# Windowed attention of a hybrid backbone: both key/value heads in one pass of 40 units, with the other input projections spread through it, and sinks in bfloat16

## The chip, the cores and the metric

One Trainium2 chip, one core of it. The metric is the device time of one execution in microseconds (us). In the text TensorE is PE (PEld for its weight loads), VectorE is DVE, ScalarE is ACT, GpSimd is POOL, and SyncE's queue, which issues every transfer here, is SP.

## The reference

512 latent tokens and 256 context tokens go through two layers of width 1024. Each layer is a SwiGLU block, a mixer and a second SwiGLU block, each behind an RMS norm with shift, scale and gate. The mixer of layer 0 is what the change is about: two kinds of attention side by side, from one input projection. Latent attention (MLA) has 8 heads; its queries, keys and values come from normalised low-rank latents through a second projection. Windowed attention has 8 query heads on 2 key/value heads; a latent query sees the context, the latent keys within 128 places and a "sink", one learned logit per head that takes part in the softmax alone:

```python
def attention_pair_mixer(h, hc, p, rope_mla, rope_win, ctx_out):
    z = h @ p["w_in"]
    ckv, kr, wk, wv, cq, wq = split_cols(z, PAIR_KV_SIZES + PAIR_Q_SIZES)
    ...
    k_a, v_a = mla_kv(ckv, kr, p, rope_mla)      # rms_norm(ckv) @ w_ukv; keys normalised per head
    o_a = dense_block_attention(mla_q(cq, p, rope_mla), ..., ...)   # rms_norm(cq) @ w_uq, norms, rotation
    o_b = window_block_attention(win_q(wq, p, rope_win), k_b, v_b, kc_b, vc_b, p["win_sink"])
    ...
# one block of window_block_attention:
    pr = softmax(concatenate([s_ctx, s_win, sink_col], axis=-1))
    o = pr[..., :n_ctx] @ vc + pr[..., n_ctx:n_ctx + 3 * BLOCK] @ vw      # the sink has no value
```

## The kernel before, in words

Nearly every product is a float32 product made of three float32r passes, so weights and operands are split into a high and a low part (`split`, L127 on ACT and L128 on DVE). Tokens stand in 6 tiles of 128: tiles 0 and 1 are context, 2 to 5 latent. The program is recorded in the order of the Python code and a scheduler of the tile layer then orders each engine's queue; each engine runs its own queue strictly in order, so where the scheduler puts an instruction decides what stands behind it.

`pair_mixer` (L715) is the mixer of layer 0. It first makes the window's keys and values and the first half of the queries, then goes through three stretches.

1. `att(0, ...)`: windowed attention of the four heads of key/value head 0. `win_attention` (L1078) makes a list of 20 units; a unit is a query tile of one head, or of two heads where the tile is context. `run_units` (L1020) issues, for unit i: the rest of unit i - 1's softmax (reciprocal L1032 on DVE, product L1035 on POOL), the "lanes" of other work, the scores of unit i, the transposes of unit i - 2's probabilities (L712), the products with the values that ended with unit i - 3 (L1158), then the copies out of PSUM (L1059, L1074), the row maximum (L1065, DVE) and the exponential (L1070, ACT). Two score buffers exist, so a pass starts and ends with units that overlap with few others.
2. `att(1, ...)`: the same for key/value head 1.
3. `mla_attention` (L1176): 40 units for the 8 latent heads. Its lane `rest` runs what is left of the query norms.

Between the units of each pass runs a background, cut in parts by `yield`: a generator tells what it has spent in its own unit of cost, and each attention unit is given a share, 3.2 in the first pass and 3.8 in the second. The first pass has `projections` (two column chunks of the input projection, norm and rotation of the second half of the window queries), the second has `latents` (L913: norms of the latents, their transposes, the products with `w_ukv` and `w_uq`, norm of the keys; its squares and its six products with 1/rms, L959, are on POOL) and the first of three `latent_queries` (L979: norm and rotation of the MLA queries of two token tiles, on DVE and POOL).

The sink enters the scores as one more product for each query tile and head, a single row of ones against two numbers of the sink row, in float32 (L1137):

```python
one = self.ones[0:1, :]
nc.tensor.matmul(out=s[:, n:n + 2], lhsT=one, rhs=sink[:, 4 * c + hd, :], start=True, stop=True)
```

There are 48 such products (24 of each key/value head), and the trace shows each as two TensorE instructions. `rsqrt` (L131) makes 1/sqrt of a small tile on DVE from a guess in integers and three Newton steps of three instructions, 11 in all; the kernel calls it 23 times, of which 8 are in this mixer. All its operands are in SBUF.

Of the kernel before, what the change touches and what calls it, by code (L numbers as in the profile page):

```python
# [8 lines left out]
F32 = mybir.dt.float32  # L9
# [13 lines left out]
T = SEQ + CTX  # L23
# [4 lines left out]
ALL_SEGS = [(0, 256), (256, 512), (512, T)]  # context tokens, latent tokens  # L28
# [3 lines left out]
class Stage:  # L32
    """A sub-layer: loads its first weights, one unit after the other, then waits for its operand."""
# [14 lines left out]
class Net:  # L48
# [28 lines left out]
    # ---- the residual: four slots that hold other things inside a mixer, while it waits in DRAM --  # L77
# [25 lines left out]
    def load_split(self, src, n, pool=None, keep=4, slots=(None, None)):  # L103
        """n columns in two halves, each as (hi, lo)"""
# [26 lines left out]
    def rsqrt(self, out, v, shape):  # L131
        """out = 1/sqrt(v) for a small positive float32 tile"""
# [3 lines left out]
        t = self.small.tile(shape, F32, tag="rs_t", name="rs_t", bufs=1)  # L136
        nc.vector.tensor_scalar(out=i, in0=v.bitcast(I32), scalar1=1, scalar2=None,
# [28 lines left out]
    def mod_finish(self, l, p):  # L166
        """bias; the scale piece becomes norm_g * (1 + scale), the FFN gates carry the 1/2"""
# [11 lines left out]
    def first_open(self, pool):  # L179
        """silu(c), silu(c_ctx) and zeros; the sum of four groups of 32 rows"""  # L180
# [14 lines left out]
    def first_product(self, pool, raw):  # L195
        """256 features of the vectors on the tensor engine, four products of 32 columns side by side"""
# [13 lines left out]
    def first_norm(self, pool, m, raw):  # L210
        """shift and scale of the first sub-layer, 128 features"""
# [7 lines left out]
    def first_gate(self, pool, i, raw):  # L219
        """half of the gate of the first sub-layer, 256 features"""  # L220
# [5 lines left out]
    def first_stats(self, pool):  # L226
        """1/rms of all tokens, on every partition"""
# [35 lines left out]
    def mod_half(self, i):  # L263
        """a half of silu(c) and of silu(c_ctx) on every partition, for the background products"""
# [35 lines left out]
    def norm_squares(self, pool, seg, order=range(KT)):  # L300
        """sum over the features of a partition of the squares"""
# [13 lines left out]
    def norm_stats(self, seg, acc):  # L315
        """1/rms of each token of the segment, on every partition (PSUM)"""
# [36 lines left out]
    def mm3(self, out, w, x, first, last):  # L353
        """out += w^T x, w = (hi, lo) stationary, x = (hi, lo) moving"""
# [17 lines left out]
    def regions(self, segs):  # L372
        """PSUM for two column tiles of each segment"""
# [72 lines left out]
    def ffn(self, l, sub, idx, segs, nxt, bg=(0, 0), first=4, start=False):  # L446
# [3 lines left out]
        # the first tiles: without the last segment, under the norm of it  # L450
# [9 lines left out]
        with st:  # L460
# [7 lines left out]
            def up(f, ss, regs=None):  # L468
                """the hidden tile f for the segments ss"""
# [13 lines left out]
            if start:  # L483
                # as the features come
# [61 lines left out]
    def seven_open(self, st, h, n0):  # L546
        """Gate and up columns (rows 1, 2) of a hidden tile against halves of the features and of the tokens,
        in seven products of halves in place of eight (Winograd's form of Strassen's)."""
# [50 lines left out]
        def start():  # L599
            """the place of the fourth block is free now"""  # L600
# [1218 lines left out]
```

## Time and profile before

| | us |
|---|---|
| device time, median of 3 runs (lowest, highest) | 2735.24 (2733.0, 2736.42) |
| span of the profiled execution, first to last instruction | 2731.1 |
| PE busy / DVE busy / ACT busy / POOL busy in that span | 2639.5 / 2171.2 / 1197.9 / 170.3 |
| mixer of layer 0, windowed attention: first score to first MLA score | 641 to 833 |
| mixer of layer 0, MLA attention | 833 to 958 |

The profiled execution's own device time is not among the three; its span stands 1.9 to 5.3 us under them, and 4.1 under their median. PE is busy 97% of the span, so nearly everywhere a microsecond counts only where PE's work gets shorter. The stretch from 641 to 833 us is the large exception: there the clock granted to PE falls and its queue waits.

### The profile page before, as it was taken

Reading aid. Unit: us, or ns where it says so; the run is one execution under the profiler, and the core shown is the slowest. Engines: PE = TensorE matmul, PEld = TensorE weight load, DVE = VectorE, ACT = ScalarE, POOL = GpSimd, SP = SyncE. Lnnn points to the kernel's source line nnn. Section 1 sums busy time; section 2 is a strip of 40 time slices with the busy share of each in tenths; the row PEclk is TensorE's granted clock in tenths of the full one; section 3 lists DMA queues with packets and bytes.
Section 4 is the critical chain, followed back from the end, with each engine's and each line's share of the span. In section 5 each row is a group of like instructions: output and inputs, shape, how many; then the busy total and the mean of one; then the engine's idle time right before and its main releaser. Section 6 shows DMA issues by size and latency. Waiting matters only on the chain. (4 is left out here: it accounts for less than half of the span.)

```text
span 2731.1 us, 44146 instructions
## 1 busy us (share of the span) xinstructions
PE 2639.5 (97%) x16848; PEld 2450.8 (90%) x16848; DVE 2171.2 (80%) x4540; ACT 1197.9 (44%) x2254; POOL 170.3 (6%) x206
## 2 busy tenths in 40 slices
PE   7999999999978899999999999999999999899999
PEld 5899999989867789999999899999998999899899
DVE  5689798977788877797989877978777677778677
ACT  4324242445656753333324542424244555534444
POOL 0000000013344300000000000000000121000000
PEclk9999999999989999999999999999999999999999
DMA  8143444431000050433433314343233112422234
GB/s 311 41 144 119 137 132 143 132 126 31 24 24 1 1 170 24 126 120 122 130 124 110 126 47 144 100 149 105 91 105 102 55 63 70 147 64 97 96 108 130
DMA packets 103461, 279.30 MB, mean 102 GB/s; under 512 B 12146, under 2 KB 15090, under 8 KB 101714
## 3 DMA queue, kind: packets, MB, share of 16 engines
q1 hardware_dynamic: 103250, 276.49, 31.3%
q8 instruction: 132, 2.16, 0.3%
q14 instruction: 79, 0.65, 0.1%
HBM read 269.11 MB, written 7.34 MB: 101 GB/s over the span
## 5 line engine op out<-in xcount | busy, mean ns | idle before, releaser
L127 ACT ACTIVATE whi<-raw 128x512 fp32r<-128x512 f32 (+3 forms) x466 | 356.0, 767 | 730.7 <-PE r L368 324.2
L128 DVE TENSOR_TENSOR wlo<-raw,whi 128x512 fp32r<-128x512 f32 (+3 forms) x466 | 400.1, 861 | 72.3 <-ACT whi L127 69.7
L596 PE MATMUL r<-t,whi 128*128 128x384 f32 (+1 forms) x1704 | 401.2, 323 | 2.8 <-DVE u L633 2.0
L596 PE MATMUL r<-hh,wlo 128*128 128x384 f32 (+1 forms) x1136 | 366.3, 323 | 0.2
L596 PE MATMUL r<-hh,whi 128*128 128x384 f32 (+1 forms) x1136 | 365.8, 322 | 0.0
L596 PE MATMUL r<-hl,whi 128*128 128x384 f32 (+1 forms) x1136 | 365.8, 322 | 0.0
L291 DVE SCALAR_TENSOR_TENSOR junk<-wm,cb 128x512 bf16<-128x512 f32 x480 | 328.8, 685 | 13.1 <-ACT cb L270 8.0
L596 PEld LDWEIGHTS r<-t,whi 128*128 128x128 f32 x1704 | 295.6, 188 | 4.5 <-DVE u L633 2.8
L596 PE MATMUL r<-t,wlo 128*128 128x384 f32 (+1 forms) x852 | 273.3, 323 | 0.2 <-DVE wlo L128 0.2
L368 PE MATMUL r<-dh,whi 128*128 128x512 f32 (+1 forms) x952 | 267.3, 345 | 0.8 <-ACT whi L127 0.8
L368 PE MATMUL r<-dh,wlo 128*128 128x512 f32 (+1 forms) x952 | 266.8, 346 | 0.3 <-DVE wlo L128 0.3
L368 PE MATMUL r<-dl,whi 128*128 128x512 f32 (+1 forms) x952 | 266.8, 344 | 0.0
L127 ACT ACTIVATE whi<-s 128x512 fp32r<-128x512 f32 x284 | 174.9, 625 | 187.5 <-DVE s L618 75.2
L596 PEld LDWEIGHTS r<-hh,wlo 128*128 128x128 f32 x1136 | 213.4, 188 | 1.3 <-DVE wlo L128 1.3
L596 PEld LDWEIGHTS r<-hl,whi 128*128 128x128 f32 x1136 | 213.4, 188 | 0.8
L596 PEld LDWEIGHTS r<-hh,whi 128*128 128x128 f32 x1136 | 213.4, 188 | 0.3
L368 PEld LDWEIGHTS r<-dh,wlo 128*128 128x128 f32 x952 | 178.6, 188 | 24.3 <-DVE wlo L128 1.1
L368 PEld LDWEIGHTS r<-dh,whi 128*128 128x128 f32 x952 | 178.0, 188 | 24.5 <-ACT whi L127 2.7
L368 PEld LDWEIGHTS r<-dl,whi 128*128 128x128 f32 x952 | 178.1, 188 | 23.5
L128 DVE TENSOR_TENSOR wlo<-s,whi 128x512 fp32r<-128x512 f32 x284 | 190.6, 683 | 2.8 <-ACT whi L127 2.1
L392 DVE SCALAR_TENSOR_TENSOR x<-r,mod,x 128x512 f32<-128x512 f32 (+1 forms) x168 | 100.0, 631 | 87.3 <-PE r L368 86.9
L596 PEld LDWEIGHTS r<-t,wlo 128*128 128x128 f32 x852 | 159.9, 188 | 0.5 <-DVE wlo L128 0.5
(403 smaller groups left out, 5880.4 us busy)
## 6 DMA issues: line engine op xcount, KB each, us to landing
raw<-gu SPq DMA_DIRECT2D x176, 512.0 KB, 4.0
wm<-w_mod SPq DMA_DIRECT2D x240, 256.0 KB, 2.9
raw<-dn SPq DMA_DIRECT2D x88, 320.0 KB, 2.9
raw<-dn SPq DMA_DIRECT2D x64, 384.0 KB, 3.1
raw<-w_out SPq DMA_DIRECT2D x28, 512.0 KB, 3.7
m<-w_mod0a SPq DMA_DIRECT2D x12, 1024.0 KB, 10.2
raw<-w_in SPq DMA_DIRECT2D x8, 512.0 KB, 4.5
raw<-w_kq SPq DMA_DIRECT2D x8, 512.0 KB, 3.6
```

The source lines that it names most:

```text
L127: self.nc.scalar.activation(out=hi, in_=src, func=AF.Copy)
L128: (e or self.nc.vector).tensor_tensor(out=lo, in0=src, in1=hi.bitcast(F32), op=ALU.subtract)
L291: nc.vector.scalar_tensor_tensor(out=junk, in0=w, scalar=1.0, in1=self.cb[:, v, :], op0=ALU.mult, op1=ALU.mult, accum_out=self.acc[:, m, v ...
L368: nc.tensor.matmul(out=outs[s][j], lhsT=w[j][wi][:, k * 128:(k + 1) * 128], rhs=xk[k][xi][:, s0:s1], start=(k == 0 and i == 0), stop=(k == ...
L392: self.nc.vector.scalar_tensor_tensor(out=self.xs[m][:, s0:s1], in0=regs[s][j], scalar=gate[:, m, v:v + 1], in1=self.xs[m][:, s0:s1], op0= ...
L596: nc.tensor.matmul(out=o, lhsT=y[wi], rhs=x[k][xi], start=first and k == 0 and i == 0, stop=last and k == H - 1 and i == 2, skip_group_che ...
```

## The change

- **One pass.** `win_attention` gets a list of 40 units, 20 for each key/value head, and one background for all of them: projections, latents and all three `latent_queries`, at a share of 2.7 a unit. The first queries of head 1 are made in the lane `tail` under the last query tile of head 0. The lane `rest` of MLA goes. The generator itself closes the pools of the first part and opens those of the latents.
- **Sink in bfloat16.** The sink is split once, by DVE, into three bfloat16 parts that stand in partitions 0, 32 and 64 of a tile of 96 that is zero elsewhere; the row of ones becomes a 96 x 128 view of the upper halves of a float32 tile of ones. The 48 products then have bfloat16 operands.
- **rsqrt** has a first step of third order (4 instructions) and a Newton step (3): 9 instructions in place of 11.

The rest of the diff takes comments away, which moves line numbers only.

```diff
@@ rsqrt
-        for _ in range(3):
-            nc.vector.tensor_tensor(out=t, in0=out, in1=out, op=ALU.mult)
-            nc.vector.scalar_tensor_tensor(out=f, in0=t, scalar=-0.5, in1=v, op0=ALU.mult, op1=ALU.mult)
-            nc.vector.scalar_tensor_tensor(out=out, in0=f, scalar=1.5, in1=out, op0=ALU.add, op1=ALU.mult)
+        nc.vector.tensor_tensor(out=t, in0=out, in1=out, op=ALU.mult)
+        nc.vector.tensor_tensor(out=f, in0=t, in1=v, op=ALU.mult)
+        stt(out=t, in0=f, scalar=-10.0 / 3.0, in1=f, op0=ALU.add, op1=ALU.mult)
+        stt(out=out, in0=t, scalar=5.0, in1=out, op0=ALU.add, op1=ALU.mult)
+        stt(out=t, in0=out, scalar=9.0 / 64.0, in1=out, op0=ALU.mult, op1=ALU.mult)
+        stt(out=f, in0=t, scalar=-3.0 / 16.0, in1=v, op0=ALU.mult, op1=ALU.mult)
+        stt(out=out, in0=f, scalar=9.0 / 16.0, in1=out, op0=ALU.add, op1=ALU.mult)
@@ pair_mixer
-            sink = ms.tile([1, 8, 2], F32, name="sink")
-            nc.sync.dma_start(out=sink, in_=ins["sink_row"])
+            sink = ms.tile([96, 8, 2], BF16, name="sink")
+            nc.vector.memset(sink, 0.0)
+            sink_f = sk.tile([96, 8, 2], F32, name="sink_f")
+            nc.sync.dma_start(out=sink_f, in_=ins["sink_row"].to_broadcast([96, 8, 2]))
+            sink_p = sk.tile([96, 8, 2], BF16, name="sink_p")
+            for r in (0, 32, 64):
+                nc.vector.tensor_copy(out=sink_p, in_=sink_f)
+                nc.vector.tensor_copy(out=sink[r:r + 1], in_=sink_p[r:r + 1])
+                if r < 64:
+                    nc.vector.tensor_tensor(out=sink_f, in0=sink_f, in1=sink_p, op=ALU.subtract)
...
-            att(0, background(projections(), 3.2))
-            prep.close()
-            self.hstack.close()
...
-                att(1, background(latents(), 3.8))
...
-                    self.mla_attention(self.pool("matt", s2), qa, kn, va, kb, gcol, oT[:2], qn[1:])
+            def background():
+                z = wq[:, :, 4:8, :]
+                yield from chunk_bg(chunk_load(1, 256), 256, z)
+                yield from self.norm_rope(pp, z, 4, window[:1])
+                yield from chunk_bg(chunk_load(4, 256), 256, zq)
+                prep.close()
+                self.hstack.close()
...
+                tabq = yield from self.latents(lp, ml, zk, zq, gain, gcol, tabs, qa, kn, va, kr, kb)
+                for t0 in (0, 2, 4):
+                    yield from self.latent_queries(lp, gain, tabq, qa, t0)
+            self.win_attention(wp, wq, kT, vs, sink, identb, band, oT[2:], in_parts(background(), 2.7))
@@ win_attention
-        one = self.ones[0:1, :]
+        one = self.ones.bitcast(BF16).rearrange("p (c two) -> p c two", two=2)[0:96, :, 1]
-        units = [(t, hd) for t in range(6) for hd in ((0, 2) if t < 2 else range(4))]
+        units = [(c, t, hd) for c in range(2) for t in range(6) for hd in ((0, 2) if t < 2 else range(4))]
-                if hd in (0, 2) and t < 5:
-                    queries(t + 1, hd // 2)
+                if hd in (0, 2) and (c, t) < (1, 5):
+                    queries(c + t // 5, (t + 1) % 6, hd // 2)
```

How the queues move, at three places. **PE, between the passes.** Before, the last products with the values (L1158, `wvs` the values) and transposes (L712 of the probabilities `pr`, L710 of the queries `wst`) of head 0 stand alone between its last score and the first score of head 1 (L1121, `wkT` the keys):

```order
L712 MATMUL t<-ident,pr 128x128 x4
L1158 MATMUL o<-pt_7585,wvs 128x256
L712 MATMUL t<-ident,pr 128x128 x3
L1158 MATMUL o<-pt_7586,wvs 128x256
```

With the change the place behind head 0's last score reads as follows (L1174 the values, L718 a transpose of the latents, L1137 the score, L1153 the sink):

```order
L718 MATMUL t<-ident,x_6231 128x128 x3
L1174 MATMUL o<-pt_7581,wvs 128x256
L1174 MATMUL o<-pt_7580,wvs 128x256
L1174 MATMUL o<-pt_7581,wvs 128x256
L718 MATMUL t<-ident,x_6231 128x128 x3
L1137 MATMUL s<-wkT,wqT 128x256 x2
L1153 LDWEIGHTS ones
L1153 MATMUL s<-sink,ones 128x2
```

From head 0's last sink product to head 1's first the program has 53 PE instructions before, and 24 with the change; scores of head 1 now stand ahead of head 0's last transposes.

**DVE, at the norm of the query latents** (`rs`, `rs_t`, `rs_f` of 128x6 are its rsqrt; L1065 the row maximum, L965 the product with 1/rms that PE's next transposes need). Before:

```order
L1065 TENSOR_REDUCE nm<-s 128x1
L142 TENSOR_TENSOR rs_t<-rs 128x48
L143 SCALAR_TENSOR_TENSOR rs_f<-rs_t,ss 128x48
L144 SCALAR_TENSOR_TENSOR rs<-rs_f,rs 128x48
L142 TENSOR_TENSOR rs_t<-rs 128x6
L143 SCALAR_TENSOR_TENSOR rs_f<-rs_t,ss 128x6
L144 SCALAR_TENSOR_TENSOR rs<-rs_f,rs 128x6
```

Two more such steps follow and then L965. With the change (L1081 the row maximum, L1090 and L1182 copies of the attention, L981 the product):

```order
L146 SCALAR_TENSOR_TENSOR rs<-rs_t,rs 128x6
L1090 TENSOR_TENSOR pt_8080<-t,pt_8079 128x512
L148 SCALAR_TENSOR_TENSOR rs_t<-rs 128x6
L1182 TENSOR_TENSOR x_6553<-o,otmp 64x128 x2
L1081 TENSOR_REDUCE nm<-s 128x1
L149 SCALAR_TENSOR_TENSOR rs_f<-rs_t,ss 128x6
L150 SCALAR_TENSOR_TENSOR rs<-rs_f,rs 128x6
L981 TENSOR_SCALAR x_6232<-x_6232,rs 128x256 x6
```

Three pieces of attention now stand inside the chain, which before had none.

**POOL, the norm of the keys** (`kn`) among the softmax products (`pr`). Before:

```order
L1035 TENSOR_SCALAR pr<-pr,rc 128x512
L1035 TENSOR_SCALAR pr<-pr,rc 128x640 x2
L959 TENSOR_TENSOR kn<-kn,rs 128x512 x6
L1035 TENSOR_SCALAR pr<-pr,rc 128x640 x3
```

With the change:

```order
L1051 TENSOR_SCALAR pr<-pr,rc 128x512 x3
L975 TENSOR_TENSOR kn<-kn,rs 128x512 x6
L128 TENSOR_TENSOR wst<-wq,wst 128x4x64
L1051 TENSOR_SCALAR pr<-pr,rc 128x512
L1051 TENSOR_SCALAR pr<-pr,rc 128x640 x5
```

The six still stand in one block in front of softmax products, three units earlier. At the end of the windowed attention little moves: between its last row maximum and the first of MLA, DVE's queue holds 69 instructions before and 62 with the change, of the same kinds of work; rsqrt's shorter form makes most of the difference. SP's queue keeps its order in the mixer, and at the program's start one of the 11 early weight tiles trades places with a modulation tile, twice.

## Rows read from the trace of the kernel before

**Rows 1.** The page's first part: busy time, share of the span, instructions.
```profile
PE 2639.5 (97%) x16848; PEld 2450.8 (90%) x16848; DVE 2171.2 (80%) x4540; ACT 1197.9 (44%) x2254; POOL 170.3 (6%) x206
```
**Rows 2.** Busy by stretch: length, PE, PEld, DVE, ACT, POOL, granted clock, DMA.
```profile
641.00:701.00 60.00, 58.70 (x457) 55.53 (x456) 46.56 (x143) 35.60 (x88) 19.74 (x31) 0.97 0.13 39
701.00:746.00 45.00, 41.85 (x258) 35.85 (x256) 29.44 (x79) 30.04 (x79) 19.74 (x31) 0.89 0.00 1
746.00:778.00 32.00, 24.11 (x129) 19.03 (x129) 25.25 (x62) 17.99 (x40) 10.38 (x12) 0.84 0.09 33
778.00:806.00 28.00, 26.30 (x185) 24.33 (x183) 21.70 (x54) 20.28 (x48) 13.85 (x14) 1.00 0.00 1
806.00:833.00 27.00, 16.20 (x66) 12.38 (x65) 26.68 (x75) 9.02 (x23) 14.59 (x15) 0.60 0.14 40
833.00:958.00 125.00, 111.15 (x774) 95.93 (x772) 105.71 (x228) 98.06 (x237) 43.73 (x56) 0.99 0.00 1
```
**Rows 3.** PE's timeline from 735.5 us: start, us, line, form, [idle before].
```profile
735.49 0.23 PE L1130 MATMUL s<-band,identb 128*128 128x128 bf16 x1
735.65 0.38 PE L1137 MATMUL s<-sink,ones 1*128 1x2 f32 x2
735.96 0.33 PE L712 MATMUL t<-ident,pr 128*128 128x128 f32 x1
```
**Rows 4.** Weight loads of sink and band: min/median/max ns, first and last start.
```profile
L1137 PEld LDWEIGHTS s<-sink,ones x96: 181/184/333, 641.0 to 806.3; 1*128 1x128 f32 x96
L1130 PEld LDWEIGHTS <-identb x48: 95/96/146, 658.2 to 806.0; 128*128 128x128 bf16 x48
```
**Rows 5.** PE's timeline between the passes, 712 to 723 us, one of its waits.
```profile
712.15 0.38 PE L1137 MATMUL s<-sink,ones 1*128 1x2 f32 x2
...
716.60 0.36 PE L1158 MATMUL o<-pt,wvs 128*128 128x256 f32 x1 [1.01 <-ACT pt L1059]
...
723.10 0.38 PE L1137 MATMUL s<-sink,ones 1*128 1x2 f32 x2
```
**Rows 6.** DVE's timeline at the norm of the query latents.
```profile
758.70 0.16 DVE L142 TENSOR_TENSOR rs_t<-rs 128x6 f32<-128x6 f32 x1
758.90 1.04 DVE L143 SCALAR_TENSOR_TENSOR rs_f<-rs_t,ss 128x6 f32<-128x6 f32 x1
...
764.97 0.17 DVE L143 SCALAR_TENSOR_TENSOR rs_f<-rs_t,ss 128x6 f32<-128x6 f32 x1
```
**Rows 7.** POOL's timeline in the same stretch.
```profile
758.87 6.04 POOL L959 TENSOR_TENSOR kn<-kn,rs 128x512 f32<-128x512 f32 x6 [1.83 <-DVE rs_t L142]
774.19 0.80 POOL L1035 TENSOR_SCALAR pr<-pr,rc 128x640 f32<-128x640 f32 x1 [9.28 <-DVE rc L1032]
```
**Rows 8.** PE's timeline in the same stretch: the wait for L965.
```profile
765.78 1.79 PE L712 MATMUL t<-ident,x 128*128 128x128 f32 x6 [5.91 <-DVE x L965]
```
**Rows 9.** POOL by line and form, 612 to 840 us: count, busy us, mean ns.
```profile
L674 POOL TENSOR_TENSOR tsq<-qa 128x512 f32<-128x512 f32 x9 | 9.5, 1061 | 6.0 <-DVE x L1166 3.1 <-ACT qa L950 1.6 <-DVE rs_i L137 1.3
L674 POOL TENSOR_TENSOR tsq<-kn 128x512 f32<-128x512 f32 x6 | 6.2, 1040 | 5.8 <-ACT kn L950 4.2 <-DVE x L1166 1.7
L959 POOL TENSOR_TENSOR kn<-kn,rs 128x512 f32<-128x512 f32 x6 | 6.0, 1042 | 1.8 <-DVE rs_t L142 1.8
```
**Rows 10.** PE's timeline at the first norm's transposes.
```profile
24.08 1.33 PE L712 MATMUL a<-ident,rstd 128*128 128x128 f32 x5 [0.46 <-DVE rstd L144]
```
**Rows 11.** PE's waits at the end of layer 1's mixer: us, count, longest.
```profile
PE c L712 <- DVE sg L1649: 4.6, 1, 4.6
```
**Rows 12.** DVE's timeline: two steps of the rsqrt in front of that last wait.
```profile
2325.18 0.16 DVE L144 SCALAR_TENSOR_TENSOR gr<-rs_f,gr 128x4 f32<-128x4 f32 x1
2325.37 0.16 DVE L142 TENSOR_TENSOR rs_t<-gr 128x4 f32<-128x4 f32 x1
```
**Rows 13.** Busy by stretch, as in rows 2, where the mixer's small inputs arrive.
```profile
520.00:550.00 30.00, 28.25 (x179) 26.11 (x179) 25.41 (x57) 13.34 (x22) 0.00 (x0) 0.94 0.54 164
```
**Rows 14.** DVE's timeline there: its wait for the transfer issued before the sink's.
```profile
529.55 0.15 DVE L727 TENSOR_SCALAR gcol<-gcol 128x1 f32<-128x1 f32 x1 [0.84 <-DMA gcol<-gain_col]
```

More of the change, by code (lines that the diff above doesn't have):

```diff
@@ L818, in pair_mixer @@
             oT = [None, None] + [self.x_slot(i, [128, 2, T]) for i in (2, 3)]
-            att = lambda c, bg: self.win_attention(wp, c, wq, kT, vs, sink, identb, band, oT[2 + c], bg)
-            def projections():
+            mls = ExitStack()
+            late = {}
+            def background():
                 z = wq[:, :, 4:8, :]
@@ L825, in projections, with in_parts @@
                 yield from chunk_bg(chunk_load(4, 256), 256, zq)
-            def background(gen, share):
+                prep.close()
+                self.hstack.close()
+                ml = self.pool("ml", mls)
+                late["qa"] = qa = ml.tile([128, 6, 8, 96], F32, name="qa")
+                late["kn"] = kn = ml.tile([128, 6, 8, 64], F32, name="kn")
+                late["va"] = va = ml.tile([128, 6, 8, 64], F32, name="va")
+                kr = ml.tile([128, 6, 32], F32, name="kr")
+                late["kb"] = kb = [[ml.tile([96, T], F32R, name=f"kb{i}{p}") for p in range(2)] for i in range(2)]
+                lp = self.pool("prep", prep)
+                tabs = lp.tile([128, 2, 4, 96], F32, name="tabs")
+                nc.sync.dma_start(out=tabs, in_=ins["rope_tab"])
+                tabq = yield from self.latents(lp, ml, zk, zq, gain, gcol, tabs, qa, kn, va, kr, kb)
+                for t0 in (0, 2, 4):
+                    yield from self.latent_queries(lp, gain, tabq, qa, t0)
+            def in_parts(gen, share):
                 left = [0.0]
@@ L836, in background @@
                 return step
[L838 to L865 removed]
+            self.win_attention(wp, wq, kT, vs, sink, identb, band, oT[2:], in_parts(background(), 2.7))
+            es2.close()
+            pso.close()
+            self.ps_o = self.pool("ps_o", pst, bufs=1, space=bass.MemoryType.PSUM)
+            self.ps_t = self.pool("ps_t", pst, bufs=3, space=bass.MemoryType.PSUM)
+            oT[0:2] = [self.x_slot(i, [128, 2, T]) for i in range(2)]
+            with ExitStack() as s2:
+                self.mla_attention(self.pool("matt", s2), late["qa"], late["kn"], late["va"], late["kb"], gcol, oT[:2])
+            prep.close()
+            mls.close()
             pst.close()
@@ L1088, in keys, with queries @@
             return max(2, t - 1), min(5, t + 1) + 1
-        def queries(t, step):
+        def queries(c, t, step):
             if step == 0:
@@ L1102, in tail, with scores @@
             if i < len(units) - 1:
-                t, hd = units[i]
-                if hd in (0, 2) and t < 5:
-                    queries(t + 1, hd // 2)
+                c, t, hd = units[i]
+                if hd in (0, 2) and (c, t) < (1, 5):
+                    queries(c + t // 5, (t + 1) % 6, hd // 2)
         def score(u):
-            t, hd = u
+            c, t, hd = u
             s = self.scores()
             if t < 2:
-                return [scores(s[:, 512 * j:512 * j + 512], t, hd + j) for j in range(2)]
-            return [scores(s, t, hd)]
-        def scores(s, t, hd):
+                return [scores(s[:, 512 * j:512 * j + 512], c, t, hd + j) for j in range(2)]
+            return [scores(s, c, t, hd)]
+        def scores(s, c, t, hd):
             w0, w1 = keys(t)
@@ L1140, in probs @@
         def probs(u):
-            t, hd = u
+            c, t, hd = u
             if hd % 2 == 0:
-                pt[t, hd // 2] = [wp.tile([128, 5, 2, 128], F32R, tag=f"pt{i}", name=f"pt{i}", bufs=2) for i in range(2)]
-            return [x if t < 2 else x[:, :, hd % 2, :] for x in pt[t, hd // 2]]
+                pt[c, t, hd // 2] = [wp.tile([128, 5, 2, 128], F32R, tag=f"pt{i}", name=f"pt{i}", bufs=2) for i in range(2)]
+            return [x if t < 2 else x[:, :, hd % 2, :] for x in pt[c, t, hd // 2]]
         def values(u):
-            t, hd = u
+            c, t, hd = u
             if t >= 2 and hd % 2 == 0:
@@ L1156, in values @@
                 v = vs[:, kt, c].rearrange("p a d -> p (a d)")
[L1157 removed]
+                for j, pp in enumerate(pt[c, t, hd // 2]):
                     nc.tensor.matmul(out=ps, lhsT=v, rhs=pp[:, i].rearrange("p h q -> p (h q)"),
@@ L1171, in win_attention, with mla_attention @@
         for step in range(2):
-            queries(0, step)
+            queries(0, 0, step)
         self.run_units(wp, units, score, probs, values, [tail, lambda i: bg()])
         bg(True)
-    def mla_attention(self, sp, qa, kn, va, kb, gcol, oT, more):
+    def mla_attention(self, sp, qa, kn, va, kb, gcol, oT):
         nc = self.nc
@@ L1260, in mla_attention @@
         queries(0, 0)
-        def rest(i):
-            for _ in more[i] if i < len(more) else ():
-                pass
-        self.run_units(sp, units, score, probs, values, [rest, tail])
+        self.run_units(sp, units, score, probs, values, [tail])
     def split_scaled(self, ps, col, hi, lo):
```

30 lines of the change are left out of this document (6 added, 24 removed).

## The prediction

> **What bounds the kernel now.** I read the page's first part, then the busy time by stretch, then the timelines of PE, DVE and POOL where the stretches show a hole. PE is busy 97% of the span [rows 1], so on the whole only shorter PE work, or a hole in PE's queue that closes, is worth time. The table by stretch [rows 2] tells where the holes are. For the windowed attention I call its five stretches A (641 to 701 us, units of head 0), B (701 to 778, in two rows), C (778 to 806) and D (806 to 833). In A, PE is busy 58.70 of 60 us at a granted clock of 0.97 (of 2.4 GHz): PE bounds it. In B it is busy 41.85 of 45 at 0.89 and then 24.11 of 32 at 0.84: neither PE nor DVE (29.44 and 25.25) fills it. C is PE's again, 26.30 of 28 at 1.00. In D, DVE is busy 26.68 of 27 us, PE 16.20 at a clock of 0.60: DVE bounds it. The MLA stage behind is balanced, 111.15 and 105.71 of 125.
>
> B has two holes. The first is the border between the passes: from head 0's last sink product at 712.15 to head 1's first at 723.10 are 11 us, in which PE runs 53 instructions and waits for the softmax of the last units (1.01 us for one copy by ACT) [rows 5]. The second is the norm of the query latents: PE waits 5.91 us for the product with 1/rms [rows 8]. DVE is late there for a reason that two timelines show side by side: a 128x6 step of rsqrt takes 0.16 to 0.17 us at 758.70 and at 764.97, but 1.04 at 758.90 [rows 6], and from 758.87 on, for 6.04 us, POOL multiplies the keys by their 1/rms [rows 7]. Both operands of these steps are in SBUF.
>
> **The change, part by part.** The sum is against the span of the profiled execution, 2731.1 us. The device times shown are about 4.1 above it by their median, which I add at the end.
>
> *Sinks.* Two PE instructions take 0.31 us from first to next work (735.65 to 735.96) [rows 3], 0.155 each; 96 weight loads of 184 ns stand behind the 48 products [rows 4]. With bfloat16 operands one instruction and one load are left. At the least the remaining one keeps its 0.155 and 0.155 is saved; at the most all 0.31. The nearest row is the bfloat16 load of the band, 95 ns [rows 4]: at that pace 0.31 - 0.095, about 0.2, which I take. Neither row shows a load that reads every second 2-byte element, as the new row of ones does; one load in place of two of 184 ns leaves no loss. 48 x 0.2 = 9.6 us, ends 7.4 and 14.9, but only where PE is the bound: 20 products are in A, 20 in B, 8 in C.
> The Trainium skill ("TensorE: Matmul & The Clock Gate", section "Weight-path perf modes") says that a load goes by columns, not by bytes. By that rule both types load alike, the step left keeps its 0.155, and the sinks give 7.4 us in place of 9.6; the trace speaks against it, 184 against 95 ns for 128 columns each.
>
> *A.* 20 x 0.2 = -4.0 (ends -3.1 and -6.2).
>
> *B.* The border goes: scores of head 1 stand ahead of head 0's last transposes, 24 instructions in place of 53 between the sinks. At the norm of the query latents, pieces of attention stand inside DVE's chain, so other units can go on meanwhile. What remains is work. PE's, at full clock: 41.85 x 0.89 + 24.11 x 0.84 = 57.5, less 20 x 0.2, is 53.5 us [rows 2]. DVE's: 29.44 + 25.25 = 54.7, less two rsqrts of two steps each at 0.19 us (the step from 2325.18 to 2325.37) [rows 12], is 53.9. Two engines so equally loaded do not overlap fully here: in the MLA stage, loaded alike, the busier is busy 89% (111.15 of 125) [rows 2]; with a chain that still has to cross three engines I take 87%: 53.9 / 0.87 = 62 us, against 77: **-15**. Ends: with A's 98% 55 us, -22; if no hole closes, the sinks alone, -4. What is late next is the row maximum and the copies on DVE, which come behind the norms.
>
> *C.* 8 x 0.2 = -1.6 (ends -1.2 and, with its 1.7 us idle as well, -4.2).
>
> *D.* The queue is DVE's and little moves: 69 instructions before, 62 now. Three rsqrts lose two steps each: 6 x 0.19 = -1.1 (ends 0, and -2.8 if two of the six are steps of 1.04 like that at 758.90 [rows 6]). Its sinks lie elsewhere and PE's clock does not matter here.
>
> *Other rsqrts.* 15 stand outside the mixer. PE waits only at two: 0.46 us for the first norm's rstd [rows 10] and 4.6 us for one at the end of layer 1's mixer [rows 11]. Two steps at each, 2 x 0.38 = -0.8 (ends 0 and -0.8). The rest lie beside PE's work, and cost or bring nothing.
>
> *Preparing the sink.* Nine small DVE instructions, at 0.16 us [rows 6] 1.5 us, where PE is busy 28.25 and DVE 25.41 of 30 us [rows 13]. They stand behind DVE's wait for the small transfer in front of the sink's, which holds it 0.84 us [rows 14]; the sink's transfer keeps its place in SP's queue, was not waited for there before, and can hold DVE half a microsecond more, with the splits of the block's weights behind it. PE's work hides most: +0.7 (ends 0 and +2).
>
> *Order of the early weight tiles, SP's queue, POOL's six products moved three units ahead, MLA without its lane.* At nothing: the early stretch has the same tiles, SP keeps its order in the mixer, and MLA's DVE queue had the queries done before its units. POOL's cover is treated as a rival.
>
> Sum: -4.0 - 15 - 1.6 - 1.1 - 0.8 + 0.7 = -21.8. Span 2709.3, time **2713.4 us**. All ends to the good: -6.2 - 22 - 4.2 - 2.8 - 0.8 = -36, 2699. All to the bad: -3.1 - 4 - 1.2 + 2 = -6, 2729.
>
> **Rivals.**
> (1) *The lock moves with the work.* POOL's six products still stand in one block, and DVE's chain for the query latents still meets them; its steps with two SBUF operands again take about 1.0 us, and PE waits as before. For it: the block is unchanged in the order, only earlier, and attention's pieces inside the chain make the chain itself longer. Against it: PE has scores of other units to run meanwhile. Then only the border closes. Its price: A runs 457 instructions in 58.70 us, 0.128 each [rows 2]; 53 at that pace are 6.8 us of the 11, so 4.2 are lost there. B gives 4.0 + 4.2 = 8.2 in place of 15, the sum is -15, and the time 2720. Chance 0.20. The Trainium skill ("SBUF — State Buffer", section "SBUF: two separate sides") has this as a rule: a DVE instruction with two SBUF inputs and a GpSimd instruction that reads SBUF exclude each other for a whole instruction. The trace agrees, 1.04 against 0.17 us.
>
> (2) *The change does not do what it says.* The order of each queue is the scheduler's, and it may let background pile up again: at the end of the windowed attention it does, 69 against 62 instructions on DVE. If DVE is behind through B and C, sinks are worth nothing there: -4.0 - 1.1 - 0.8 + 0.7 = -5, 2730. Chance 0.10.
>
> (3) *Slower: POOL comes in front of the softmax.* POOL does squares and products of the keys and squares of the queries, 6.2 + 6.0 + 9.5 = 21.7 us [rows 9], and the product that ends each unit's softmax is on POOL behind them. Now the block costs no softmax product anything: before the next one, at 774.19, POOL sat idle for 9.28 us [rows 7]. In one pass with two score buffers, each microsecond by which such a product comes late can hold the transposes, then the buffers, then PE. B's holes would stay, and the rest give -4.0 - 4.0 - 1.6 - 1.1 - 0.8 + 0.7 = -11. It decides from 11 of the 21.7 us on the path; with all of them 2735 - 11 + 21.7 = 2746. Against it: POOL is busy only 10.38 of 32 and 13.85 of 28 us in the last stretches. Chance 0.06.
>
> (4) *Better:* B as full as A is now, -22, and C and D at their good ends: about 2702 or below. Chance 0.06.
>
> The forecast has the remaining 0.58.
>
> **How the numbers follow.** The likeliest case gives 2713.4. Its own spread, with (1) inside, is 2700 to 2728. The range goes to 2731 so that it takes in (2); outside are (3), half of (4) and some of the unknown in what the scheduler does elsewhere. A measurement of this kernel tells about 0.2% from no change, 5.5 us, so faster means under 2729.8: the forecast, (1) and (4), 0.84. No change is (2), and the part of (3) that stays small: 0.11. Slower is the rest, 0.05.
>
> **What the changed profile would show.** Sink products as 48 rows, one load each of about 95 ns, and 0.1 us from a sink to the next work. From head 0's last sink to head 1's first 2 to 4 us, not 11. PE's wait for the product with 1/rms (5.91) well below 3, and the granted clock of the stretch up from 0.84. From the first score of the windowed attention to the first of MLA 170 us in place of 192; in it a DVE-bound tail still of some 26 us at a low clock; MLA again 125. If the sink's load shows 184 ns, the sinks gave 7.4. If the wait for 1/rms is still 5 us or more, (1) holds. If PE waits for DVE's row maxima all along, (2). If POOL's softmax product is what transposes wait for, several microseconds each time, (3). Wrong altogether would be a gain outside 641 to 833 us of more than some 2 us, since I have priced nothing else.

## The result, and the profile after

The changed kernel takes 2709.64 us by the median of 4 runs (2705.19 to 2711.18), the kernel before, measured beside it, 2734.12. The ratio is 0.9916, with a 95% interval of 0.9900 to 0.9932: 19 to 27 us faster. The forecast was 2713.4 in a range of 2700 to 2731. The sum holds; the experiments show that its terms do not.

The page's first part for the changed kernel, against [rows 1]: PE has 22 us less to do, DVE 10.

```profile
PE 2617.1 (97%) x16800; PEld 2435.1 (90%) x16800; DVE 2161.1 (80%) x4503; ACT 1196.9 (44%) x2254; POOL 171.6 (6%) x206
```

The next four stretches start and end at the same instruction in both kernels, though the background is spread differently over them. The busy time by stretch (columns as in [rows 2]) of the kernel before: units of head 0 with the border, units of head 1, the end behind the last sink product, and MLA from its first to its last score.

```profile
641.00:723.10 82.10, 77.66 (x583) 71.79 (x582) 61.17 (x183) 48.67 (x123) 26.14 (x42) 0.96 0.10 29
723.10:806.30 83.20, 73.60 (x443) 63.18 (x443) 62.08 (x152) 55.23 (x131) 37.58 (x45) 0.90 0.04 13
806.30:832.70 26.40, 15.60 (x63) 11.86 (x63) 26.08 (x74) 8.92 (x23) 14.29 (x15) 0.60 0.14 41
832.70:947.60 114.90, 104.20 (x727) 90.41 (x726) 99.09 (x214) 91.02 (x223) 42.22 (x54) 0.99 0.00 1
```

The same four of the changed kernel:

```profile
638.90:707.10 68.20, 63.51 (x529) 60.02 (x527) 55.72 (x167) 44.07 (x112) 25.60 (x41) 0.97 0.11 34
707.10:787.00 79.90, 68.04 (x451) 59.97 (x450) 63.93 (x160) 58.07 (x142) 38.00 (x46) 0.91 0.04 14
787.00:811.00 24.00, 14.15 (x61) 11.06 (x59) 23.76 (x68) 8.59 (x22) 14.21 (x16) 0.64 0.14 45
811.00:925.50 114.50, 103.59 (x729) 89.71 (x728) 98.79 (x215) 91.66 (x222) 42.35 (x54) 1.00 0.00 1
```

The three stretches of the windowed attention fall from 191.7 to 172.1 us, MLA keeps its length. That is 19.6 of the 24.4 us between the two spans (2731.1 and 2706.7); 4.8 lie outside the windowed attention, where the prediction had priced about nothing.

PE's timeline of the changed kernel around a sink product and at the border of the heads (start, us, line, form):

```profile
701.47 0.23 PE L1146 MATMUL s<-band,identb 128*128 128x128 bf16 x1
701.54 0.17 PE L1153 MATMUL s<-sink,ones 96*128 96x2 bf16 x1
701.57 0.31 PE L718 MATMUL t<-ident,pr 128*128 128x128 f32 x1
...
703.78 0.17 PE L1153 MATMUL s<-sink,ones 96*128 96x2 bf16 x1
...
707.15 0.18 PE L1153 MATMUL s<-sink,ones 96*128 96x2 bf16 x1
```

From the band's product to the work behind the sink it is 0.10 us where it was 0.47 (735.49 to 735.96 in [rows 3]): 0.37 a sink. A sink product with no band in front gives as much: at the start of head 1 the sinks follow one another every 0.37 us (707.15, 707.52) where it was 0.74 (723.10, 723.84). The next work starts 0.03 to 0.05 us behind the sink's start where nothing is waited for, though the sink's weights take 100 ns to load: PE's load of them stands under the product ahead (PE's weight loads, grouped, from 638 to 790 us: count, busy us, mean ns):

```profile
L1153 PEld LDWEIGHTS <-ones 96*128 96x128 bf16 x48 | 4.9, 102 | 0.7
L1146 PEld LDWEIGHTS <-identb 128*128 128x128 bf16 x48 | 4.8, 100 | 1.5
```

The border, 11 us from sink to sink in [rows 5], is 3.4 us. DVE's timeline at the norm of the query latents, against [rows 6]:

```profile
733.70 1.04 DVE L144 TENSOR_TENSOR rs_f<-rs_t,ss 128x6 f32<-128x6 f32 x1
734.78 0.97 DVE L145 SCALAR_TENSOR_TENSOR rs_t<-rs_f 128x6 f32<-128x6 f32 x1
735.78 0.97 DVE L146 SCALAR_TENSOR_TENSOR rs<-rs_t,rs 128x6 f32<-128x6 f32 x1
737.27 0.48 DVE L148 SCALAR_TENSOR_TENSOR rs_t<-rs 128x6 f32<-128x6 f32 x1
```

DVE's steps are as slow as before, but PE no longer waits for the product behind them: it has scores and products of the key latents to run. What it waits for instead, from 638.9 to 787 us, is above all DVE's copies of the probabilities out of PSUM (us, count, longest):

```profile
PE t L718 <- DVE pt L1090: 7.4, 10, 1.7
PE s L1137 <- ACT pr L1086: 2.3, 4, 0.8
```

The longest of these waits is at the slow steps themselves: the copy stands in DVE's queue right behind the three of about 1 us (DVE's timeline, then PE's).

```profile
736.66 0.68 DVE L1090 TENSOR_TENSOR pt<-t,pt 128x512 fp32r<-128x512 f32 x1
737.40 0.33 PE L718 MATMUL t<-ident,pr 128*128 128x128 f32 x1 [1.68 <-DVE pt L1090]
```

So of PE's wait of 5.91 us at this norm 1.7 are left, for another operand.

### The profile page after: what moved, and what is told of

Its sections match the earlier page's. It is cut to its first block, busy times and chain, and to the rows that moved or that the text cites. A ratio compares the mean times of both kernels' runs of the same rounds, so it can differ in the third digit from the quotient of the medians.

```text
span 2706.7 us, 44030 instructions
## 1 busy us (share of the span) xinstructions
PE 2617.1 (97%) x16800; PEld 2435.1 (90%) x16800; DVE 2161.1 (80%) x4503; ACT 1196.9 (44%) x2254; POOL 171.6 (6%) x206
## 5 line engine op out<-in xcount | busy, mean ns | idle before, releaser
L374 PEld LDWEIGHTS r<-dh,wlo 128*128 128x128 f32 x952 | 178.6, 188 | 24.4 <-DVE wlo L128 1.1
```

Of the source, the lines that this page charges most:

```text
L374: nc.tensor.matmul(out=outs[s][j], lhsT=w[j][wi][:, k * 128:(k + 1) * 128], rhs=xk[k][xi][:, s0:s1], start=(k == 0 and i == 0), stop=(k == ...
```

## The experiments

The change has three parts, so the first six runs make all their combinations: S is the sinks in bfloat16, R the short rsqrt, P the one pass. Each was timed against the kernel before, on the same chip as it; the twelve runs below were made on three chips, so kernels are compared by their ratios.

| kernel | label | median, us | ratio (95% interval) | us by the ratio |
|---|---|---|---|---|
| S | e1_two_sinkb | 2726.7 | 0.9985 (0.9976, 0.9993) | -4 |
| R | e2_two_rsqrt | 2719.2 | 0.9964 (0.9952, 0.9977) | -10 |
| P | e3_one_alone | 2730.71 | 0.9995 (0.9986, 1.0005) | -1 |
| P, R | e4_one_sinkf | 2722.77 | 0.9970 (0.9960, 0.9980) | -8 |
| S, R | e5_two_both | 2716.14 | 0.9941 (0.9929, 0.9953) | -16 |
| S, P | e6_one_oldrsqrt | 2722.27 | 0.9960 (0.9946, 0.9974) | -11 |
| S, R, P | the change | 2709.64 | 0.9916 (0.9900, 0.9932) | -23 |

The last column is the ratio less one, times 2732. Each has an interval of 2 to 4 us to either side, so a difference of two of them is good to about 5 us.

**S alone**, the kernel before with the change's preparation of the sink and

```diff
-            sink = ms.tile([1, 8, 2], F32, name="sink")
+            sink = ms.tile([96, 8, 2], BF16, name="sink")
...
-        one = self.ones[0:1, :]
+        one = self.ones.bitcast(BF16).rearrange("p (c two) -> p c two", two=2)[0:96, :, 1]
```

> The kernel before with the sinks in bfloat16 alone (two passes, old rsqrt). Theory (the prediction's terms): 48 sinks at 0.2 us less 0.7 for the preparation, -9 us, about 2725. Rival, from the changed kernel's trace, where the step from a band product to the work behind the sink fell from 0.47 to about 0.1 us: 0.36 a sink, up to 17.5 us, of which those in the stretches that PE bounds count, so -13 to -17, about 2719; then one pass is worth much less than the 10 us or so that the prediction leaves it.

Neither: -4. Its profiled execution, the shortest of the eleven, takes less time from first to last sink product, 152.6 us in place of 165.3, with PE busy 129.74 us in place of 151.26; but in two passes PE then waits longer for the product with 1/rms, 8.6 us where it was 5.9 [rows 8], and 6.2 us for the exponentials:

```profile
PE t L712 <- DVE x L976: 8.6, 1, 8.6
PE s L1132 <- ACT pr L1081: 6.2, 5, 3.3
```

The first ten microseconds of MLA gave another part back in that execution (the end behind the last sink product, then MLA's first 10 us):

```profile
794.50:817.90 23.40, 14.80 (x61) 11.06 (x59) 23.00 (x72) 8.47 (x23) 11.94 (x13) 0.58 0.16 46
817.90:827.90 10.00, 9.01 (x30) 7.13 (x31) 8.90 (x19) 3.98 (x11) 6.50 (x8) 0.50 0.00 1
```

The changed kernel's first 10 us of MLA:

```profile
811.00:821.00 10.00, 8.93 (x56) 7.15 (x54) 8.86 (x23) 7.03 (x17) 4.38 (x6) 1.00 0.00 1
```

PE is as busy in both, and runs 30 instructions at the lower level of its clock (1.2 GHz) where it runs 56 at the higher. The engine came from a stretch in which it was busy 14.80 of 23.40 us in one, 14.15 of 24.00 in the other; what decides between them no run here shows. Single executions of a kernel lie up to 12 us apart (the kernel before: 2726.11 to 2737.79 among 19). A difference of 3 or 4 us between two traces proves nothing here; terms are read from the ratios.

**R alone**, the kernel before with the nine-instruction rsqrt of the diff.

> The kernel before with the shorter rsqrt alone. Theory: -0.8 in front of PE's two waits outside the mixer, -0.8 of DVE work at the norms of the second stretch, -1.1 in the tail that DVE bounds: -2.7, about 2731.5. Rival: all of it lies beside other work and the time is that of before within 1 us. DVE 46 instructions fewer in both.

Both fall: -10, four times the theory. This was the largest surprise, and the two runs e9 and e10 below are for it.

**P alone**, the changed kernel with the sinks in float32 and the old rsqrt.

> The one pass alone (float32 sinks, old rsqrt). Theory: of the 15 us of stretch B, 11 are not sinks; with little else -10 to -11, about 2724. Rival (sinks carry most of the result): -5, about 2729. A third: float32 sinks on a fuller PE eat what the border gives, 0.

The one pass alone is worth 1 us, with an interval across zero: the third view. PE's wait for the product with 1/rms is gone from its list. But the time from first to last sink product falls only from 165.3 to 159.2 us:

```profile
641.40:800.60 159.20, 146.78 (x1024) 132.43 (x1023) 125.29 (x337) 102.87 (x253) 64.21 (x86) 0.96 0.07 22
```

PE is busy 146.78 of it, 92%, so it is nearly the bound itself, with float32 sinks on its path. And a new hole stands where the wait for 1/rms was. POOL's six products of the keys run there from 746.12 to 752.17, and DVE's steps take about 1 us each meanwhile. Only behind them come a softmax product (POOL, to 752.84) and a copy out of PSUM (DVE, to 753.32), and PE's next transposes wait 3.42 us (POOL's timeline, then PE's, which names the DVE step that ended last):

```profile
752.14 0.70 POOL L1034 TENSOR_SCALAR pr<-pr,rc 128x512 f32<-128x512 f32 x1
753.47 1.09 PE L712 MATMUL t<-ident,pr 128*128 128x128 f32 x4 [3.42 <-DVE rs_f L143]
```

The next run, P and R, has a wait of 4.41 us at the same place. No run tells how much of the missing worth is this hole and how much is PE's own work.

**P and R**, the changed kernel with the sink put back to float32.

> The changed kernel with the sinks put back to float32 (one pass, short rsqrt). Theory: 48 x 0.2 less 0.7 comes back, +9 against the changed kernel, about 2719. Rival: 0.36 a sink, +13 to +17, about 2725. If sinks and one pass hinder each other, this and the run with the sinks alone do not add up to the same.

The rival's size: 2722.77 against 2709.64, and by the ratios 15 us come back. The sinks are worth 15 us in this company and 4 alone, so the parts hinder or help each other, as the last sentence allowed.

**S and R**, two passes.

> Two passes with the bfloat16 sinks and the short rsqrt, so all of the change but the one pass. Theory (the two parts add up, and the one pass is worth little, as its run alone says): -5.7 and -13.2 of the runs alone make -19, about 2713.5, and one pass is left with some 4 us of the whole change. Rival (the prediction's size of the one pass, or that it needs the other two): 10 us or more are left to it, so this kernel is at 2720 or above.

-16, near the theory: its -19 came from medians, by the ratios the two runs alone make 4 + 10 = 14. 7 us are left to the one pass, between theory and rival.

**S and P**, the changed kernel with the old rsqrt.

> The changed kernel with the old rsqrt. Theory (the short rsqrt is worth its 13 us in any company): about 2722. Rival (its 13 us in two passes were partly the place at which the clock falls, and not its instructions): it is worth the 2.7 us of the prediction, about 2712. By the stretches outside the mixer, where its runs were 5 us shorter, at least those come back: 2715.

The theory: 2722.27. The short rsqrt is worth 10, 12, 7 and 12 us in its four companies.

**The lock at the norm of the query latents.** The changed kernel with

```diff
-            nc.gpsimd.tensor_tensor(out=kn[:, t], in0=kn[:, t], in1=self.bcast(r[:, t], 64), op=ALU.mult)
+            nc.vector.tensor_tensor(out=kn[:, t], in0=kn[:, t], in1=self.bcast(r[:, t], 64), op=ALU.mult)
```

> The changed kernel with the six products of the keys with 1/rms on DVE in place of POOL. If DVE's steps of the query latents' rsqrt are held by these products (0.97 to 1.04 us where 0.17 is usual), all of them are at 0.16 to 0.2 us now; DVE pays about 6 x 0.65 = 3.9 us for the products and gets about 4 us back: 0 +- 2 on the time. Rival (the long steps have another cause, such as their small shape or a wait): they stay near 1 us, DVE has 4 us more, and the time is 2 to 4 us longer.

DVE's timeline of this kernel at the same place:

```profile
731.09 3.69 DVE L975 TENSOR_TENSOR kn<-kn,rs 128x512 f32<-128x512 f32 x6
734.70 0.15 DVE L144 TENSOR_TENSOR rs_f<-rs_t,ss 128x6 f32<-128x6 f32 x1
736.71 0.16 DVE L145 SCALAR_TENSOR_TENSOR rs_t<-rs_f 128x6 f32<-128x6 f32 x1
737.92 0.16 DVE L146 SCALAR_TENSOR_TENSOR rs<-rs_t,rs 128x6 f32<-128x6 f32 x1
```

All steps behind the six products are at 0.15 to 0.17 us: the long ones were POOL's doing, as the theory has it. The Trainium skill ("SBUF — State Buffer", section "Who interferes with whom") gives the rule, an exclusive lock between a DVE instruction with two SBUF inputs and a GpSimd instruction that reads SBUF; the trace agrees, 0.16 against 0.97. The time is that of the changed kernel, 2709.71. This does not show that nobody waits for the chain: DVE pays 3.69 us for the six products, and PE's wait of 1.68 us for the copy behind the steps is still 1.02 here. What the lock costs in one pass is therefore not shown by this run; with float32 sinks it stands in the waits of 3.42 and 4.41 us above.

**Squares of the MLA queries on ACT**, the changed kernel with

```diff
-                                      [2, 16], True)
+                                      [2, 16])
```

> The changed kernel with the squares of the MLA queries on ACT in place of POOL (nine, 9.5 us on POOL). Theory (the end of the windowed attention is bound by DVE, which POOL's squares and products hold up): ACT has room (8.6 of 24 us), DVE's instructions with two operands in SBUF get shorter by some 3 us, and the time falls by 2 to 4 us, under 2708. Rival: the squares on ACT stand in front of the exponentials and the copies of the transposes, which PE and DVE wait for, and it is 2 us slower or more.

2708.97, ratio 0.9916, the changed kernel's own: neither. From last sink product to first MLA score it is 21.1 us in place of 24.0, from first to last sink product 153.3 in place of 148.1. The end is shorter by the 3 us of the theory, and the units are longer; the execution profiled is this kernel's slowest, so not all of their 5 us need be the edit's.

**Where the rsqrt's time is.** Two kernels with both forms of rsqrt, the short one called in one place or the other (`rsqrt_short` is the nine-instruction form):

```diff
-        self.rsqrt(rstd, ms, [128, nt])
+        self.rsqrt_short(rstd, ms, [128, nt])
...
-        self.rsqrt(rstd[:, :nt], ms[:, :nt], [128, nt])
+        self.rsqrt_short(rstd[:, :nt], ms[:, :nt], [128, nt])
...
-        self.rsqrt(r, ss, [128, 4])
+        self.rsqrt_short(r, ss, [128, 4])
```

> The kernel before with the short rsqrt only at the 15 calls outside the windowed mixer (norms of the sub-layers, gates of layer 1). Theory, from the lengths of the stretches outside the mixer in four traces with and four without it: -7 us, about 2725 (the start of the program and the first products behind it -4, the norm in front of layer 1's first products -2, layer 1's mixer -2, and 1 or 2 given back). Rival (the prediction): only two waits of PE see it, -0.8, about 2732.

2723.88, ratio 0.9973 (0.9962 to 0.9984): -7 us, the theory. The other eight calls, the kernel before with

```diff
-        self.rsqrt(r, ss, [128] + shape)
+        self.rsqrt_short(r, ss, [128] + shape)
```

> The kernel before with the short rsqrt only at the 8 calls of the windowed mixer. Theory: the prediction's -1.9, with the granted clock's luck -1 to -4, about 2730; with the run of the other 15 calls it adds up to the -10 to -13 of the run with all of them. Rival (the 13 us come from the mixer, where the run with all of them was 10 us shorter): -8 or more, about 2724.

2728.85, ratio 0.9989 (0.9978 to 1.0000): -3 us, the theory. The two add up to the -10 of both. PE's waits in layer 1's mixer, 2136.4 to 2365.5 us of the kernel before, show a part of it:

```profile
PE c L712 <- DVE sg L1649: 4.6, 1, 4.6
PE f L356 <- DVE gv L1449: 1.6, 1, 1.6
PE b L368 <- ACT o L127: 1.5, 1, 1.5
PE b L368 <- ACT sg L1523: 1.0, 1, 1.0
```

and of the changed kernel, 2113.6 to 2340.2:

```profile
PE c L718 <- DVE sg L1661: 4.2, 1, 4.2
PE b L374 <- ACT o L127: 1.5, 1, 1.5
PE o L362 <- ACT ah L127: 0.8, 1, 0.8
PE b L374 <- ACT sg L1535: 0.6, 1, 0.6
```

Only the first of these four names a tile close behind an rsqrt, and it gives the 0.4 us that the prediction counted; the wait of 1.6 for `gv` goes altogether, others shrink. `gv` is a split of values which no norm feeds: before, two splits of `o` (3.66 us) stand right ahead of it in DVE's queue, and with the short rsqrt at the outer calls alone the scheduler has put a split of `k` between the two. DVE sits idle twice between the last rsqrt and these splits (1.86 and 2.28 us), so that wait went with the order and not with shorter steps. The stretch as a whole (starts from PE's timelines, in the kernels without R: before, S, P, S and P; and with it: R, S and R, P and R, the change) tells more than the list:

| PE's stretch, in the times of the kernel before | without R | with R |
|---|---|---|
| 120.3 to 201.4: first hidden tiles of the first block | 81.2, 80.7, 80.8, 81.1 | 79.9, 79.3, 79.3, 79.4 |
| 1535.2 to 1618.1: norm ahead of layer 1's first block, its first products | 82.9, 82.6, 83.3, 85.5 | 81.6, 81.4, 81.2, 81.7 |
| 2136.4 to 2365.5: layer 1's mixer to the next norm | 229.1, 229.7, 230.6, 229.2 | 226.0, 225.8, 227.7, 226.6 |
| 2365.5 to 2433.7: that norm, first products behind it | 68.2, 68.6, 68.4, 69.5 | 70.8, 71.2, 71.2, 69.1 |

The columns do not overlap but in the last row, where a part is given back: about -1.5, -2 and -3, then +2. The two runs of this section agree: the outer calls alone give 79.5, 81.3, 225.5 and 68.9, the inner ones alone 80.6, 82.5, 231.0 and 68.5. The start of the program, up to 120.3, takes 118.7 to 120.3 us without R and 115.2 to 119.0 with it, with too much scatter for a number. Outside layer 0's mixer four of PE's waits differ most between these two runs, 5.0 us together: for `u`, the sums of a SwiGLU block, 1.9 (inner calls) and 0.2 (outer calls), for `gv` 1.6 and none, for `hl`, the low part of a normalised operand, 1.2 and 0.3, and for a weight's high part `whi` 0.8 and none. Smaller ones go and come. With the short rsqrt at the outer calls the scheduler also lets two of the first block's weight tiles pass a modulation tile in SP's queue; in the kernel with the inner calls it does not. What of the 7 us is this new order of the queues, and what the two DVE steps themselves, was not tried apart.

**The small preparations on POOL.** The waits of PE from 510 to 565 us show the price of preparing the sink. Before, and in the changed kernel:

```profile
PE b L368 <- DVE dl L128: 1.2, 1, 1.2
```

```profile
PE b L374 <- DVE dl L128: 2.3, 1, 2.3
```

The split `dl` of the last hidden tile stands in DVE's queue behind the two transfers [rows 14] and now behind six of the nine instructions for the sink, about 1 us. The edit, two of seven lines alike:

```diff
-            nc.vector.tensor_scalar(out=gain[:, 0:64], in0=gain[:, 0:64], scalar1=64 ** -0.5, scalar2=None, op0=ALU.mult)
+            nc.gpsimd.tensor_scalar(out=gain[:, 0:64], in0=gain[:, 0:64], scalar1=64 ** -0.5, scalar2=None, op0=ALU.mult)
...
-                nc.vector.tensor_copy(out=sink_p, in_=sink_f)
+                nc.gpsimd.tensor_copy(out=sink_p, in_=sink_f)
```

> The changed kernel with the mixer's small preparations (gain, its column, the identity in bfloat16, the three parts of the sink) on POOL, which stands idle then, in place of DVE. Theory: PE's wait for the split of the last hidden tile there (2.3 us, of which the sink's instructions made 1.1 and DVE's waits for two transfers the rest) goes: -2.3, about 2707. Rival (the products behind wait for weights or for the norm anyway): the wait moves on and the time stays at 2709 to 2710.

2707.16 (2703.2 to 2708.34), ratio 0.9906 (0.9893 to 0.9919): 2.5 us below the changed kernel, as forecast, though the two intervals overlap, so the times alone do not separate them. PE's wait does:

```profile
PE b L374 <- DVE dl L128: 0.5, 1, 0.5
```

This is the fastest kernel of the study.

**An earlier background**, that kernel with

```diff
-            self.win_attention(wp, wq, kT, vs, sink, identb, band, oT[2:], in_parts(background(), 2.7))
+            self.win_attention(wp, wq, kT, vs, sink, identb, band, oT[2:], in_parts(background(), 3.5))
```

> As the last, and the background gets a share of 3.5 a unit in place of 2.7, so that the norms of the MLA queries stand between the last units and no longer behind the last one: 29 DVE instructions stand between the last window row maximum and the first of MLA, where there were 62. Theory (the end is long because DVE works there alone): of its 24 us 10 go, the units take some 5 of them back, and the clock stays up into MLA: -5 against the last kernel, about 2702. Rival (DVE is the bound of the units as well): the units grow by what the end loses, +-1; a second: the projections come too early and hold the units of the first head, slower by 3 or more.

2710.86, 3.7 us slower than the last, the time of the second rival; the stretches show something of both. Its two stretches, first to last sink product and from there to the first MLA score:

```profile
637.20:796.40 159.20, 136.81 (x979) 123.45 (x978) 137.53 (x368) 102.43 (x253) 74.32 (x96) 0.89 0.09 28
796.40:810.50 14.10, 8.95 (x64) 6.90 (x61) 10.45 (x32) 8.27 (x23) 3.44 (x5) 1.00 0.01 2
```

and of the last kernel:

```profile
637.50:785.40 147.90, 129.45 (x977) 117.69 (x977) 119.71 (x326) 102.27 (x253) 63.67 (x86) 0.97 0.07 23
785.40:809.50 24.10, 13.79 (x59) 10.59 (x59) 23.92 (x69) 8.51 (x22) 14.50 (x16) 0.65 0.15 45
```

The end is shorter by the 10 us that were expected, and the units longer by 11, as the first rival has it; half of that lies in the units of the first head (74.5 us from its first sink product to head 1's, where it was 68.6), as the second has it. DVE is busy 144 and 148 us of the 172 and 173, PE 143 and 146. With the two so equally full over the windowed attention as a whole, moving DVE's work from the end into the units moves PE's hole and does not close it. The clock is in it too: granted 0.89 in the units where it was 0.97, with PE busy 7 us more for the same products.

## Why the prediction was right, and which of its terms were not

**The sum.** -21.8 was forecast, -23 measured. By the four companies in the table (with and without each of the other two parts) the mean worth of a part is: sinks (4 + 6 + 10 + 15) / 4 = 9, rsqrt (10 + 12 + 7 + 12) / 4 = 10, one pass (1 + 7 - 2 + 7) / 4 = 3. From the intervals of the table each mean is good to about 2 us. The prediction had 9.6 - 0.7 = 8.9 for the sinks, 0.8 + 1.1 + 0.8 = 2.7 for the rsqrt and 10 for the one pass. So two errors of 7 us canceled, and that the sum came out so near was luck.

**The sinks.** "At that pace 0.31 - 0.095, about 0.2" was too little: the load taken as the pace of the remaining step is hidden under the product ahead, and the band's product ahead is freed too, 0.16 to 0.07. A sink gives 0.37 us, above the upper end of 0.31. (The rows have 19, 21 and 8 of them in A, B and C; 20, 20 and 8 were taken.) From first to last sink product PE's work at full clock falls from 151.26 x 0.93 = 141 to 131.54 x 0.94 = 124 us: 17 for 48. Half of that reached the time, on average: 4 and 6 us in two passes, where PE then waits at the norm (8.6 us in S alone), 10 and 15 in one. The Trainium skill ("TensorE: Matmul & The Clock Gate", section "LDWEIGHTS (loading the stationary operand)") says that the number of rows does not count in a load: here 96 rows and 128 rows of bfloat16 agree, 102 and 100 ns. The type does count: a float32 load of one row took 184 [rows 4], and those of 128 rows that stand beside the sinks in the changed kernel take about 190 to 210.

**B.** The border closed as forecast, 11 to 3.4 us, and the wait of 5.9 is gone but for 1.7 us in another place; "what is late next" was right too: DVE's copies, 7.4 us. The step that failed is the division by 0.87 as if it were the one pass's own worth. It needs PE's work to shrink as well: with float32 sinks, the one pass is worth 1 and -2 us, with bfloat16 sinks 7 and 7, a difference of 6 and 9 whose mean, 7 or 8 give or take 4, is clear of zero. Sinks and one pass together are worth 11 us with the old rsqrt and 23 - 10 = 13 with the short one, where the prediction had 19 for the two. By stretch, in one trace of each kernel: head 0's units give 6 us, the border 8, head 1's units 3 and the end 2, where 4.0 were forecast for A (all but the last of head 0's units), 15 for B, 1.6 for C and 1.1 for D. What B lacks is in head 1's units, where DVE now has 160 instructions in place of 152.

**Other rsqrts.** "PE waits only at two" is the step that failed most. It searched PE's waits for those that name a tile of the rsqrt, and found two. Waits that name other tiles (the normalised operand's split, the sums of a SwiGLU block, a split of values) shrink as well, and the queues are ordered anew. 0.8 us was 7. How the 7 divide between the shorter chain and the new order stays open.

**Preparing the sink.** +0.7, with an end of +2: 1.1 us of PE's wait, at the instruction that the text named, the splits behind DVE's waits.

**D and C.** The end behind the last sink is 24.0 us in place of 26.4, -2.4 where -1.1 was taken with an end of -2.8; DVE fills it as before (23.76 of 24.00). The eight sinks of C cannot be told apart from B in the new order.

**The rivals.** (1) is half right: the lock moves along, 0.97 to 1.04 us a step, and PE has other work in front of the product with 1/rms, but not in front of every copy behind the steps: 1.68 us of wait are left of 5.91, and more with float32 sinks (3.42 and 4.41). (2) holds for the end alone. (3) did not come in the changed kernel: in its units PE's list has no wait of over 0.2 us for POOL. It was near, though. Up to 724.77 transposes wait 2.21 us, for a softmax product that POOL, busy with squares of the keys, ends at 723.74, and for a copy that ACT ends at 724.63 and that so decides. And in the one pass alone a softmax product stood behind the six products, as (3) has it, at the wait of 3.42. The prediction's own test, a gain of over 2 us outside 641 to 833, did come out against it: 4.8 in the two traces, and the 7 of the outer calls confirm it.

## What to carry to other kernels

A part's worth depends on its company: a product that is cheap to shorten is worth little while its engine has holes, and closing the holes is worth little while that product fills them; so price both together, or run all the combinations before crediting one. A shorter chain can be felt at what stands behind it on its engine's queue, and its edit can order the queues anew, so a count of the waits that bear its name is a lower bound; a run with the edit at some of its places tells where the time is. Where two engines are nearly equally full over a whole stage, moving one's work from the end into the middle may only move the hole, as it did here.

## What the runs showed that was not expected

A matmul with two columns costs PE 0.03 to 0.05 us of its queue when its weights are bfloat16, and 0.31 in float32 with a one-row operand: the 100 ns load of the former is hidden, the two loads of 184 ns of the latter, which overlap, fill nearly all of the 0.31. A block of POOL products between the steps of a DVE chain can be paid for by a copy behind it on DVE's queue, and not by the chain's own consumer alone: the copy at 736.66 came behind three steps of 1.04, 0.97 and 0.97 us. Behind a stretch in which PE was busy about 60% of the time, the clock's lower level could last into the next stretch for 10 us in one execution and for none in another, with PE equally busy in both: 30 instructions in 10 us against 56.
